# Regrouping the convolution taps, the fold and the norm in the hybrid attentions of a four-layer kernel

## Chip, cores and metric

The kernel runs on one core of one Trainium2 chip. The metric is the device time of one execution in microseconds; a time is the median of several runs. A profile is one execution on the chip, recorded by the hardware.

## What is computed

The reference applies two stacks of two layers each to 1024 tokens of width 1024, all in float32. The change is in the first stack, the hybrid layers. One hybrid layer normalizes its input, projects it to 15 slices, and mixes four groups of 256 channels:

```python
y_a = conformer_conv(a_u, a_v, conv_a_w, conv_a_b, ln_a_g, ln_a_b) * jax.nn.silu(a_z)
y_b = short_gated_conv(b_b, b_c, b_x, conv_b_w) * jax.nn.silu(b_z)
y_c = window_gqa(...) * jax.nn.silu(c_z)
y_d = neighborhood_attn(...) * jax.nn.silu(d_z)
y = jnp.concatenate([y_a, y_b, y_c, y_d], axis=-1)
return x + jnp.einsum("bse,ed->bsd", y, w_out)
```

`conformer_conv` is a depthwise convolution of width 31 over tokens, followed by a layer norm over the 256 channels and a silu. `short_gated_conv` has width 3. `window_gqa` is attention with four query heads over 128 tokens to each side, `neighborhood_attn` attention with four heads over a two-dimensional window of 8 x 16 keys. The second stack (retention, differential attention, feed-forward) is not touched.

## The kernel before

Activations lie channel-major: tiles of 128 channels x 1024 tokens. A float32 matmul operand is split in two parts (`hi`, `lo`), and a product takes three matmuls. `dense` is one projection of 128 output channels: two loads of weights (SP issues the DMA, L202), each split by ScalarE (L205) and GpSimd (L194), then 48 matmuls of 512 columns (L222, L224, L225) into two banks of the ring `pa` of three, which an `evac` function empties. Such a unit needs only the layer's input, so it can stand between other work.

`hybrid` writes one layer in this order: the sliding-window attention `swa`, in which `conv_a` computes the input `h` of the wide convolution for two channel tiles c; the neighbourhood attention `na` for its two pairs of heads; the gate projections; `conv_b`, the short convolution; further gates; the residual and the output projection (`residual`, `hybrid_out`), whose second half needs the normed convolution and `na`'s result.

An attention runs over groups of 256 queries: `swa` has 16 groups, each call of `na` has eight (two heads j, four groups g), so a layer has 32. A group makes scores on TensorE (L507, or L334 and L335) into the two banks `ps`; VectorE adds the mask and takes the maximum (L511, L591); ScalarE takes the exponential (L514, L599); VectorE inverts the sum (L517, L601); GpSimd scales the rows (`scale`, L446). `pv` transposes the rows on TensorE (L416), ScalarE copies them to SBUF (L419), VectorE makes the rest (L420), and TensorE multiplies with the values (L427) into the one bank `po`. `fold` adds the two halves of that bank: a copy on ScalarE (L441), an add on VectorE (L442), and a store by SP (L443).

The wide convolution has 30 taps for each channel tile after its first. For c = 0 a tap is one VectorE instruction over 1024 tokens (L696). For c = 1 it is four pieces of 256 tokens: ScalarE makes a product (L700) in one of two tiles `prod`, and GpSimd adds it (L701). `self.taps` alternates between the two, and `some_taps(n)` writes the next n. `swa` writes three after each group's fold, `na` two. `conv_a_norm` (L716 to L738) writes what taps are left and the layer norm; it is called between the two heads of the second `na`. The pool `cc` has four tiles, for h and the sums of both channel tiles; `conv_b` takes its h and y (L756 to L763) from the same pool.

The order of each engine's queue is not this text's alone. The framework plans the queues at build time, and the order of writing is a rank in that plan:

```python
with tile.TileContext(nc, schedule_with_timeline_sim=True) as tc:
```

At run time each engine works through its queue in the planned order and waits on semaphores.

Of the kernel before, what the change touches and what calls it, by code (L numbers as in the profile page):

```python
# [21 lines left out]
ALU = mybir.AluOpType  # L22
AX = mybir.AxisListType

P = 128
# [39 lines left out]
NPRM = C_FN2 + 8  # L65


NTAP0, NTAP = 3, 2
NGATE = 4
RM = 2  # L70
CPW = 256


class Builder:
    def __init__(self, nc, tc, a, es):
        self.nc, self.tc, self.a, self.es = nc, tc, a, es
        self.n = 0
        self.pools = {}
        self.put_off = None
        self.ready, self.use_ready = [], False  # L80
        self.open(es, cp=1, rp=1, wp=3, xp=13, dp=6, sp=8)
        self.open(es, bass.MemoryType.PSUM, pa=3, ps=2, pt=2, po=1)
        self.open(es, bass.MemoryType.DRAM, dr=2)
# [351 lines left out]

    def fold(self, y, j, g, O):

        nc = self.nc
        m, c = slice(64 * j, 64 * j + 64), slice(64 - 64 * j, 128 - 64 * j)
        t = self.tl("sp", (P, 256), tag="fold", bufs=2)  # L440
        nc.scalar.copy(t[m], O[c, 0:256])  # L441
        nc.vector.tensor_tensor(t[m], O[m, 0:256], t[m], ALU.add)  # L442
        nc.sync.dma_start(y[m, g * 256:(g + 1) * 256], t[m])  # L443

    def scale(self, out, src, colm):
        self.nc.gpsimd.tensor_scalar(out, src, colm, 1.0, ALU.mult, ALU.mult)  # L446
# [23 lines left out]
    def swa(self, l, w):  # L470
        nc = self.nc
# [13 lines left out]
        accs = self.conv_a(l, w)  # L485
        ys = []
        for c in range(2):
# [4 lines left out]
            for j in range(2):  # L492
# [4 lines left out]
                for g in range(4):  # L497
                    p = self.tl("p", (P, 2, 3 * P + 1))
                    nc.vector.tensor_copy(p[:, :, 0], sink.to_broadcast([P, 2]))
                    st = self.st(6)  # L500
                    for e in range(2):
                        i = 2 * g + e
                        k0, k1 = max(i - 1, 0), min(i + 2, NT)
                        n = (k1 - k0) * P
                        ps = self.psS()
                        for m in range(2):
                            nc.tensor.matmul(ps[:, :n], qs[:, j, i * P:(i + 1) * P],  # L507
                                             kk[c][:, m, k0 * P:k1 * P], start=(m == 0),
                                             stop=(m == 1))
                        m0 = (k0 - (i - 1)) * P  # L510
                        nc.vector.tensor_tensor_reduce(  # L511
                            p[:, e, 1:1 + n], ps[:, :n], self.swam[:, m0:m0 + n], -0.125, sink,
                            ALU.add, ALU.min, st[:, e:e + 1])
                        nc.scalar.activation(p[:, e, 0:1 + n], p[:, e, 0:1 + n], AF.Exp,  # L514
                                             scale=-1.0, bias=st[:, e:e + 1],
                                             accum_out=st[:, 2 + e:3 + e])
                    nc.vector.reciprocal(st[:, 4:6], st[:, 2:4])  # L517
                    for e in range(2):
                        i = 2 * g + e
                        n = (min(i + 2, NT) - max(i - 1, 0)) * P  # L520
                        self.scale(p[:, e, 1:1 + n], p[:, e, 1:1 + n], st[:, 4 + e:5 + e])
                    i = 2 * g
                    blocks = [(i, [0, 1]), (i + 1, [0, 1])]
                    if i > 0:
                        blocks.append((i - 1, [0]))
                    if i + 2 < NT:
                        blocks.append((i + 2, [1]))

                    def src(q, kt):
                        o = 1 + (kt - max(i + q - 1, 0)) * P  # L530
                        return p[:, q, o:o + P]

                    O = self.psO()
                    self.pv(O, blocks, src, vops)
                    self.fold(y, j, g, O)
                    self.some_taps(NTAP0)
            ys.append(y)
        return ys, accs


# [16 lines left out]
        nc.vector.memset(t[64:128, 14, :], -BIG)  # L557
        return t

    def na(self, l, w, c, between=None):  # L560
        nc = self.nc
        qf = self.proj(w, 20 + c)
        kf = self.proj(w, 22 + c)
# [2 lines left out]
        V = self.v_pair(vf)  # L566
        y = self.yspill()
        for j in range(2):
            if j and between is not None:
                between()  # L570
            tb = self.na_bias(l, 2 * c + j)
            for g in range(4):
                ps_ = []
# [40 lines left out]
                def src(q, kt):  # L614
                    o = (kt - ps_[q][1]) * P
                    return ps_[q][0][:, o:o + P]

                O = self.psO()
                self.pv(O, blocks, src, V(j))
                self.fold(y, j, g, O)  # L620
                self.some_taps(NTAP)
        return y


# [68 lines left out]
    def tap(self, h, acc, t, w, c):  # L693
        nc = self.nc
# [1 line left out]
            nc.vector.scalar_tensor_tensor(acc, h[:, t:t + S], w, acc, ALU.mult, ALU.add)  # L696
            return
        for i in range(0, S, CPW):
            q = self.tl("sp", (P, CPW), tag="prod", bufs=2)
            nc.scalar.activation(q, h[:, t + i:t + i + CPW], AF.Copy, scale=w)  # L700
            nc.gpsimd.tensor_tensor(acc[:, i:i + CPW], acc[:, i:i + CPW], q, ALU.add)  # L701

# [75 lines left out]
    def hybrid(self, l, last):  # L778
# [3 lines left out]
        with contextlib.ExitStack() as es:  # L782
            self.open(es, pj=4, p=4, tp=4, kl=1, nab=1, cc=4)
            self.open_klo()
            yc, accs = self.swa(l, w)
            yd = [self.na(l, w, 0), self.na(l, w, 1, lambda: self.conv_a_norm(l, accs))]
            gc = [self.gate_spill(w, 18 + c) for c in range(2)]
            yb = self.conv_b(l, w)
            gd = [self.gate_spill(w, 26 + c) for c in range(2)]
            self.spilled = yb  # L790
# [937 lines left out]
```

## Time and profile before

| what | value |
|---|---|
| timed runs | 3733.79 us median of 3 (3724.83 to 3737.05) |
| profiled execution, its own time | 3726.09 us |
| its span, first to last instruction | 3724.3 us |
| mean granted TensorE clock | 0.962 of full speed |
| layer 0: first tap on VectorE, last add of a tap on GpSimd | 97.2 and 298.0 us |

The span is that of the one profiled execution. Times inside it are counted from its first instruction. PE is TensorE's matmul, PEld its weight load, DVE VectorE, ACT ScalarE, POOL GpSimd, SP the queue that issues DMAs. A granted clock of 1.00 is 2.4 GHz, 0.50 is 1.2 GHz.

### The profile page before, as it was taken

How to read it: one execution, taken by the hardware profiler on the slowest of the kernel's cores; microseconds unless marked ns; L12 is line 12 of the kernel's file. 1: busy time of each engine (PE TensorE's matmuls, PEld its weight loads, DVE VectorE, ACT ScalarE, POOL GpSimd, SP SyncE). 2: the span in 40 equal slices, each digit the busy share in tenths (PEclk: the TensorE clock that was granted, in tenths of full speed). 3: DMA queues.
4: the chain of work that ended last, by engine and by line, in shares of the span. 5: the costliest groups of instructions: out<-in, count | busy, mean ns of one | idle time of the engine just before them, and what ended most of it. 6: DMA issues, size and time to landing. Idle time of an engine off the chain costs nothing.

```text
span 3724.3 us, 46324 instructions
## 1 busy us (share of the span) xinstructions
PE 3433.5 (92%) x15872; PEld 2808.6 (75%) x15872; DVE 2531.2 (68%) x3963; ACT 1573.2 (42%) x3207; POOL 2119.8 (57%) x1891
## 2 busy tenths in 40 slices
PE   8899999999999998879999899999997789999898
PEld 6788887788888777667777677887776667777676
DVE  6856647655656655677766899665555586677997
ACT  4475433764444443252333344454433433333333
POOL 4785555874553333466666788533334466666884
PEclk9999999999999998889999999999998889999999
DMA  4112531123422323542122333221236422212432
GB/s 130 36 57 58 177 121 54 39 59 106 156 75 50 52 65 68 149 147 82 68 74 88 119 117 94 88 53 45 48 83 147 122 82 74 96 69 80 144 94 85
DMA packets 186060, 330.40 MB, mean 89 GB/s; under 512 B 49504, under 2 KB 60128, under 8 KB 185824
## 3 DMA queue, kind: packets, MB, share of 16 engines
q1 hardware_dynamic: 185824, 327.44, 29.5%
q8 instruction: 125, 2.05, 0.3%
q14 instruction: 111, 0.91, 0.1%
HBM read 250.23 MB, written 73.99 MB: 87 GB/s over the span
## 4 chain that ended last, share of the span: by engine, by line
PE 60%; DVE 14%; DMA 11%; POOL 7%; issue 4%; ACT 3%; SPq 0%; DVEq 0%; POOLq 0%; ACTq 0%
PE pa L222 9%; PE pa L225 9%; PE pa L224 9%; PE pa L1132 3%; DMA y<-ho 3%; PE pa L1134 3%; PE pa L1135 3%; PE po L427 3%; PE T L1135 3%; PE T L1132 2%; PE T L1134 2%; POOL wlo L194 2%; POOL cc L701 2%; PE ps L1132 2%; PE ps L1135 2%
## 5 line engine op out<-in xcount | busy, mean ns | idle before, releaser
L222 PE MATMUL pa<-xp,whi 128*128 128x512 f32 x2048 | 821.1, 402 | 18.8 <-ACT xp L189 9.9
L224 PE MATMUL pa<-xp,whi 128*128 128x512 f32 x2048 | 820.5, 401 | 8.4 <-DVE xp L190 8.3
L225 PE MATMUL pa<-xp,wlo 128*128 128x512 f32 x2048 | 821.0, 401 | 0.2 <-POOL wlo L194 0.2
L194 POOL TENSOR_TENSOR wlo<-raw,whi 128x512 fp32r<-128x512 f32 x304 | 430.7, 1417 | 447.6 <-ACT whi L205 443.8
L194 POOL TENSOR_TENSOR wlo<-xp,whi 128x512 fp32r<-128x512 f32 x248 | 359.8, 1454 | 190.0 <-ACT whi L1208 189.5
L222 PEld LDWEIGHTS pa<-xp,whi 128*128 128x128 f32 x2048 | 394.2, 193 | 95.5 <-ACT xp L189 10.8
L224 PEld LDWEIGHTS pa<-xp,whi 128*128 128x128 f32 x2048 | 393.3, 192 | 88.4 <-DVE xp L190 14.1
L225 PEld LDWEIGHTS pa<-xp,wlo 128*128 128x128 f32 x2048 | 393.8, 192 | 77.7 <-POOL wlo L194 0.7
L1208 ACT CAST whi<-xp 128x512 fp32r<-128x512 f32 x248 | 153.8, 620 | 405.0 <-PE pa L1134 139.3
L1132 PE MATMUL pa<-xp,whi 128*128 128x512 f32 x672 | 273.8, 407 | 49.8 <-DVE xp L1097 10.9
L205 ACT CAST whi<-raw 128x512 fp32r<-128x512 f32 x304 | 186.9, 615 | 233.8 <-PE pa L224 147.3
L1135 PE MATMUL pa<-xp,wlo 128*128 128x512 f32 x672 | 269.2, 403 | 5.8 <-POOL wlo L194 5.4
L1134 PE MATMUL pa<-xp,whi 128*128 128x512 f32 x672 | 269.5, 401 | 0.0
L446 POOL TENSOR_SCALAR p<-p,st 128x256 f32<-128x256 f32 (+4 forms) x224 | 157.3, 710 | 196.1 <-DVE st L991 94.2
L701 POOL TENSOR_TENSOR cc<-cc,prod 128x256 f32<-128x256 f32 x240 | 199.8, 854 | 30.0 <-ACT prod L700 23.8
L1132 PEld LDWEIGHTS pa<-xp,whi 128*128 128x128 f32 x672 | 130.8, 195 | 91.9 <-issue 19.6
L420 DVE TENSOR_TENSOR tp<-T,tp 128x512 fp32r<-128x512 f32 (+2 forms) x224 | 132.2, 599 | 97.4 <-ACT tp L419 96.4
L334 PE MATMUL ps<-xp,xp 128*128 128x512 f32 (+4 forms) x384 | 144.1, 376 | 37.7 <-DVE p L932 31.9
L427 PE MATMUL po<-tp,xp 128*128 128x256 f32 (+1 forms) x1024 | 166.5, 283 | 12.4 <-ACT tp L419 11.3
L427 PEld LDWEIGHTS po<-tp,xp 128*128 128x128 f32 x1024 | 151.3, 193 | 33.3 <-ACT tp L419 16.2
L700 ACT ACTIVATE prod<-cc,c 128x256 f32<-128x256 f32 x240 | 119.0, 507 | 108.8 <-POOL cc L701 97.3
L986 ACT ACTIVATE p<-p,st 128x384 f32<-128x384 f32 (+3 forms) x192 | 117.1, 611 | 111.8 <-DVE st L979 110.2
(316 smaller groups left out, 8241.4 us busy)
## 6 DMA issues: line engine op xcount, KB each, us to landing
raw<-w_in SPq DMA_DIRECT2D x208, 256.0 KB, 2.9
xp<-x SPq DMA_DIRECT2D x48, 512.0 KB, 6.8
xp<-w_gate SPq DMA_DIRECT2D x44, 512.0 KB, 5.2
xp<-w_up SPq DMA_DIRECT2D x44, 512.0 KB, 5.1
raw<-w_out SPq DMA_DIRECT2D x80, 256.0 KB, 3.3
x<-xp SPq DMA_DIRECT2D x80, 256.0 KB, 2.2
h<-xp SPq DMA_DIRECT2D x40, 512.0 KB, 2.9
xp<-h SPq DMA_DIRECT2D x80, 256.0 KB, 4.4
```

The lines of the kernel that those rows point to most:

```text
L194: self.last_rest = self.nc.gpsimd.tensor_tensor(lo, src, hi.bitcast(F32), ALU.subtract)
L205: nc.scalar.copy(hi, raw)
L222: nc.tensor.matmul(ps[h], hi[:, k - k0, :], x[:, 0, t], start=(k == 0), stop=False)
L224: nc.tensor.matmul(ps[h], hi[:, k - k0, :], x[:, 1, t], start=False, stop=False)
L225: nc.tensor.matmul(ps[h], lo[:, k - k0, :], x[:, 0, t], start=False, stop=(k == nk - 1))
L427: nc.tensor.matmul(O[:, qs[0] * P:qs[0] * P + w], lhsT, pt[part][:, o:o + w], start=((kt, qs) == blocks[0] and i == 0), stop=((kt, qs) == ...
L446: self.nc.gpsimd.tensor_scalar(out, src, colm, 1.0, ALU.mult, ALU.mult)
L701: nc.gpsimd.tensor_tensor(acc[:, i:i + CPW], acc[:, i:i + CPW], q, ALU.add)
L1132: nc.tensor.matmul(ps, hi[:, k, :], xh, start=(start and k == 0), stop=False, skip_group_check=True)
L1134: nc.tensor.matmul(ps, hi[:, k, :], xl, start=False, stop=False, skip_group_check=True)
L1135: nc.tensor.matmul(ps, lo[:, k, :], xh, start=False, stop=(k == len(ops) - 1), skip_group_check=True)
L1208: self.nc.scalar.copy(hi, src)
```

## The change

Both attentions write two taps a group instead of three and two, and write them between the scaling and `pv` instead of after the fold. `fold` writes only ScalarE's copy; the add and the store are kept back and written by `fold_rest` ahead of the next group's `pv`, or at the end of the attention. The norm moves from between the heads of the second `na` to behind the first two gates. The product tiles become four. The same instructions are written, in another order.

```diff
@@ -65,7 +65,7 @@
 NPRM = C_FN2 + 8
 
 
-NTAP0, NTAP = 3, 2
+NTAP = 2
 NGATE = 4
 RM = 2
 CPW = 256
@@ -77,6 +77,7 @@
         self.n = 0
         self.pools = {}
         self.put_off = None
+        self.fold_off = None
         self.ready, self.use_ready = [], False
         self.open(es, cp=1, rp=1, wp=3, xp=13, dp=6, sp=8)
         self.open(es, bass.MemoryType.PSUM, pa=3, ps=2, pt=2, po=1)
@@ -435,12 +436,22 @@
 
     def fold(self, y, j, g, O):
 
+
         nc = self.nc
         m, c = slice(64 * j, 64 * j + 64), slice(64 - 64 * j, 128 - 64 * j)
         t = self.tl("sp", (P, 256), tag="fold", bufs=2)
         nc.scalar.copy(t[m], O[c, 0:256])
-        nc.vector.tensor_tensor(t[m], O[m, 0:256], t[m], ALU.add)
-        nc.sync.dma_start(y[m, g * 256:(g + 1) * 256], t[m])
+
+        def rest():
+            nc.vector.tensor_tensor(t[m], O[m, 0:256], t[m], ALU.add)
+            nc.sync.dma_start(y[m, g * 256:(g + 1) * 256], t[m])
+
+        self.fold_off = rest
+
+    def fold_rest(self):
+        if self.fold_off is not None:
+            self.fold_off()
+        self.fold_off = None
 
     def scale(self, out, src, colm):
         self.nc.gpsimd.tensor_scalar(out, src, colm, 1.0, ALU.mult, ALU.mult)
@@ -530,11 +541,13 @@
                         o = 1 + (kt - max(i + q - 1, 0)) * P
                         return p[:, q, o:o + P]
 
+                    self.some_taps(NTAP)
+                    self.fold_rest()
                     O = self.psO()
                     self.pv(O, blocks, src, vops)
                     self.fold(y, j, g, O)
-                    self.some_taps(NTAP0)
             ys.append(y)
+        self.fold_rest()
         return ys, accs
 
 
@@ -557,7 +570,7 @@
         nc.vector.memset(t[64:128, 14, :], -BIG)
         return t
 
-    def na(self, l, w, c, between=None):
+    def na(self, l, w, c):
         nc = self.nc
         qf = self.proj(w, 20 + c)
         kf = self.proj(w, 22 + c)
@@ -566,8 +579,6 @@
         V = self.v_pair(vf)
         y = self.yspill()
         for j in range(2):
-            if j and between is not None:
-                between()
             tb = self.na_bias(l, 2 * c + j)
             for g in range(4):
                 ps_ = []
@@ -615,10 +626,12 @@
                     o = (kt - ps_[q][1]) * P
                     return ps_[q][0][:, o:o + P]
 
+                self.some_taps(NTAP)
+                self.fold_rest()
                 O = self.psO()
                 self.pv(O, blocks, src, V(j))
                 self.fold(y, j, g, O)
-                self.some_taps(NTAP)
+        self.fold_rest()
         return y
 
 
@@ -696,7 +709,7 @@
             nc.vector.scalar_tensor_tensor(acc, h[:, t:t + S], w, acc, ALU.mult, ALU.add)
             return
         for i in range(0, S, CPW):
-            q = self.tl("sp", (P, CPW), tag="prod", bufs=2)
+            q = self.tl("sp", (P, CPW), tag="prod", bufs=4)
             nc.scalar.activation(q, h[:, t + i:t + i + CPW], AF.Copy, scale=w)
             nc.gpsimd.tensor_tensor(acc[:, i:i + CPW], acc[:, i:i + CPW], q, ALU.add)
 
@@ -783,8 +796,9 @@
             self.open(es, pj=4, p=4, tp=4, kl=1, nab=1, cc=4)
             self.open_klo()
             yc, accs = self.swa(l, w)
-            yd = [self.na(l, w, 0), self.na(l, w, 1, lambda: self.conv_a_norm(l, accs))]
+            yd = [self.na(l, w, 0), self.na(l, w, 1)]
             gc = [self.gate_spill(w, 18 + c) for c in range(2)]
+            self.conv_a_norm(l, accs)
             yb = self.conv_b(l, w)
             gd = [self.gate_spill(w, 26 + c) for c in range(2)]
             self.spilled = yb
```

## Rows read from the trace of the kernel before

**Rows 1.** The page: busy time, share, instructions of each engine.

```profile
PE 3433.5 (92%) x15872; PEld 2808.6 (75%) x15872; DVE 2531.2 (68%) x3963; ACT 1573.2 (42%) x3207; POOL 2119.8 (57%) x1891
```

**Rows 2.** Busy us by stage: stretch, its length, engines (instructions), clock, DMA.

```profile
core 0: us, PE busy (x) PEld busy (x) DVE busy (x) ACT busy (x) POOL busy (x), PEclk, DMA share, GB/s
125.00:200.00 75.00, 65.24 (x321) 53.03 (x320) 53.61 (x103) 48.10 (x116) 69.30 (x76) 0.98 0.12 34
...
200.00:400.00 200.00, 199.58 (x1072) 169.72 (x1071) 114.90 (x263) 124.43 (x269) 129.21 (x161) 1.00 0.24 67
...
625.00:710.00 85.00, 74.56 (x367) 61.18 (x367) 61.98 (x116) 51.80 (x124) 74.14 (x79) 0.98 0.11 33
```

**Rows 3.** The same view in windows of 10 us.

```profile
140.00:150.00 10.00, 6.63 (x23) 5.03 (x23) 7.71 (x12) 5.22 (x14) 9.72 (x10) 0.83 0.13 34
...
190.00:200.00 10.00, 9.59 (x51) 7.86 (x50) 6.88 (x17) 7.08 (x20) 8.04 (x12) 1.00 0.14 39
...
650.00:660.00 10.00, 7.61 (x33) 6.25 (x34) 7.73 (x16) 5.13 (x14) 9.72 (x8) 0.83 0.10 31
```

**Rows 4.** Timeline of TensorE: start, us, what, idle before and releaser.

```profile
138.69 0.39 PE L225 MATMUL pa<-xp,wlo 128*128 128x512 f32 x1
...
139.83 0.39 PE L224 MATMUL pa<-xp,whi 128*128 128x512 f32 x1
...
142.46 0.77 PE L507 MATMUL ps<-xp,xp 128*128 128x256 f32 x2 [2.24 <-DVE st L511]
...
143.02 0.63 PE L225 MATMUL pa<-xp,wlo 128*128 128x512 f32 x1
```

**Rows 5.** Waits from 125 to 200: us in total, times, longest.

```profile
ACT prod L700 <- POOL cc L701: 27.7, 24, 3.1
DVE st L517 <- ACT p L514: 9.9, 7, 2.9
...
PE ps L507 <- DVE st L511: 6.2, 4, 2.4
...
DVE fold L442 <- ACT fold L441: 5.6, 3, 3.0
...
PE po L427 <- ACT tp L419: 2.5, 2, 1.4
```

**Rows 6.** Chain of waits from 125 to 176, shares by line.

```profile
by line: POOL cc L701 46.3%; POOL p L446 26.0%; POOL wlo L194 14.2%; issue 6.6%; DVE cc L696 3.2%; ACT prod L700 2.8%; ACT p L514 1.2%; DVE p L511 1.0%; POOLq L194 0.2%; DVE st L511 0.0%
```

**Rows 7.** Source lines: count, ns min/median/max, first and last start.

```profile
L696 DVE SCALAR_TENSOR_TENSOR cc<-cc,c,cc x30: 1264/1285/2315, 97.2 to 167.1; 128x1024 f32<-128x1024 f32 x30
...
L701 POOL TENSOR_TENSOR cc<-cc,prod x120: 719/741/1772, 123.1 to 298.0; 128x256 f32<-128x256 f32 x120
...
L441 ACT COPY fold<-po x6: 364/370/371, 143.6 to 197.4; 64x256 f32<-64x256 f32 x6
```

**Rows 8.** GpSimd's busy us of L701 alone, then of L446 alone (twice).

```profile
125.00:200.00 75.00, 40.69 (x46) 0.98 0.12 34
...
125.00:200.00 75.00, 18.50 (x20) 0.98 0.12 34
...
200.00:300.00 100.00, 13.13 (x20) 1.00 0.20 57
```

**Rows 9.** Source line of the fold's add in layer 0.

```profile
L442 DVE TENSOR_TENSOR fold<-po,fold x32: 394/422/429, 144.0 to 478.4; 64x256 f32<-64x256 f32 x32
```

**Rows 10.** Source lines: norm, residual, output, second convolution (both layers).

```profile
L716 PE MATMUL T<-cc,c x8: 590/592/595, 394.2 to 401.8; 128*128 128x512 f32 x8
...
L738 DVE SCALAR_TENSOR_TENSOR cc<-p,cc x4: 671/676/692, 414.7 to 433.7; 128x512 f32<-128x512 f32 x4
...
L822 DVE TENSOR_TENSOR xp<-pa,xp x16: 672/684/692, 438.0 to 489.4; 128x512 f32<-128x512 f32 x16
...
L838 DVE TENSOR_TENSOR xp<-pa,xp x16: 691/692/692, 492.1 to 532.9; 128x512 f32<-128x512 f32 x16
...
L761 ACT ACTIVATE cc<-cc,c x4: 1152/1153/1157, 299.5 to 836.5; 128x1024 f32<-128x1024 f32 x4
```

**Rows 11.** Groups of TensorE from 298 to 394: count, busy us, mean ns.

```profile
L225 PE MATMUL pa<-xp,wlo 128*128 128x512 f32 x97 | 38.4, 396 | 0.0
```

## The prediction

> **What bounds the kernel now.** The page first: TensorE is busy for 92% of the span [rows 1], so a change that adds and removes no arithmetic can only win what TensorE stands still or runs slowly. The profiled execution took 3726.09 us with a span of 3724.3; the three timed runs have a median of 3733.79, 7.7 above it. I make the sum against 3726.09 and carry the difference to the median. A change under 0.3% (11.2 us) can't be told from none here.
>
> Next, busy time by stage of the two hybrid layers [rows 2]. In layer 0 TensorE is busy for 65.24 of the 75 us from 125 to 200, then for 199.58 of 200. Layer 1 repeats it: 74.56 of 85 from 625 to 710. So of all that the diff touches, only the first groups of the sliding-window attention have idle to give: 9.76 and 10.44 us, 20.2 together. In that stretch GpSimd is busy for 69.30 of 75.
>
> The finer windows [rows 3] show the clock as well: 0.83 granted in 140 to 150 and in 650 to 660, where TensorE stands still for 3.37 and 2.39 us. In the timeline, matmuls of 512 columns take 0.39 us before a 2.24 us stop and 0.63 behind it [rows 4]: 2.4 GHz, then 1.2 for a while. That is 0.17 x 10 = 1.7 us per layer, 3.4 in all.
>
> Then who is waited for there [rows 5]. TensorE waits 6.2 us for VectorE's masked maximum (L511, the reader of the score banks) and 2.5 for ScalarE's copy of a transpose (L419). VectorE waits 9.9 for the exponential (L514), and ScalarE waits 27.7 us, 24 times, in L700, the product of a tap, for GpSimd's add L701 to give back one of two product tiles. Engines run their queues in order, so an exponential or a copy behind L700 waits too. The chain of waits from 125 to 176 agrees: 46.3% L701, 26.0% the scaling L446, 14.2% the weight split L194 [rows 6]. GpSimd's queue sets the pace of these groups.
>
> **The change, part by part.** No instruction is added or removed: 30 taps on VectorE and 30 on ScalarE and GpSimd (120 products, 120 adds) per layer remain.
>
> *Taps, three to two a group in the sliding window.* Taps alternate between the channels, so three a group are on average 1.5 x 4 = 6 adds, two are 4. Six fold copies lie in 125 to 200 [rows 7], five intervals of a group; the last ends in 190 to 200, where GpSimd is busy for only 8.04 of 10 [rows 3]. That leaves four intervals in which it sets the pace: 4 x 2 = 8 adds fewer ahead of the scalings. An add costs 40.69 / 46 = 0.885 us in this stretch [rows 8]. 8 x 0.885 = 7.1 us per layer, 14.2 for two. The bounds: nothing, if the queues are ordered by what is ready and the adds stay where they are; and all idle and slow clock, 20.2 + 3.4 = 23.6. I take 14.2, which leaves the clock uncounted, since one stop left over can keep it slow. What goes out comes back later: the window's 16 groups give up 16 taps to the neighbourhood attention, eight of them on GpSimd: 32 adds, or 24 us at the 0.741 us of the median one [rows 7]. The cover there is TensorE's full queue: from 200 to 400 GpSimd is busy for only 129.21 of 200 us [rows 2]. Uncovered they would cost those 24.
>
> *Four product tiles.* ScalarE may run two more products ahead: 2 x 0.74 = 1.5 us of slack, against waits of 27.7 / 24 = 1.2 us on average, 3.1 at most [rows 5]. I count nothing for it: it frees ScalarE, not GpSimd, which is the pace. Its bounds are the whole ScalarE part, already within 23.6, and the loss in the third rival.
>
> *Fold in two steps.* VectorE's add (0.42 us, 32 a layer) and its store go behind the next group's scores [rows 9]. VectorE waits 5.6 us in this stretch for the fold copy [rows 5], standing in front of L511; that wait overlaps the same stops, so it is not added. Nothing to 2 x 5.6 us. What is late: the single output bank is released later, so the next group's value matmuls (L427) can wait behind the add; a group's interval of about 10 us hides 0.42. On SP the stores move past weight loads, 32 a layer; SP is no step of the chain [rows 6], and their readers come a stage later, so nothing; were a weight load held up by a store that waits for the add, the price is that add's lateness, a group at most. The fold has two tiles, and one is held a group longer, with as much slack.
>
> *Norm behind the gates.* It now stands behind both halves of the second neighbourhood attention instead of between them. Its matmuls start at 394.2 and its last VectorE step at 433.7 [rows 10], 40 us of chain. The cover is the residual's dense work, whose evacuations run from 438.0 to 489.4, before the first of the output's at 492.1 [rows 10]. If the two change places, the norm ends about where attention now ends, at 478.4 [rows 9]. The output's first matmuls, 24 x 0.228 = 5.5 us ahead of their evacuation, need it by 487. I take nothing; each us past that is lost once per layer, 40 at the most without cover.
>
> **Sum.** 3726.1 - 14.2 = 3711.9 for an execution like the profiled one; against the median 3733.8 - 14.2 = 3719.6, say 3720.
>
> **Rivals.** *Same: GpSimd stays the pace, because VectorE's taps slow it.* All 30 VectorE taps are issued between 97.2 and 167.1, while the sixth group is folded at 197.4 [rows 7]; in program order six groups hold 18 taps, nine of them VectorE's. So instructions are placed by readiness, and the written place of a tap hardly counts. While those taps run, GpSimd's work stretches: 20 scalings take 18.50 us against 13.13 for 20 in the next 100 us [rows 8], though some of the latter are wider; 46 adds take 40.69 against 34.1 at the median [rows 7, 8]. That is 5.4 + 6.6 = 12 us per layer, more than the whole idle. If this is the cause, moving GpSimd's taps wins nothing: 3734. By the Trainium skill, page "SBUF — State Buffer", section "Who interferes with whom", a VectorE instruction with two inputs in SBUF contends with a GpSimd one that reads SBUF, and whichever issues second waits for the first to finish. The 18.50 against 13.13 us [rows 8] agree with it. Against the rival: taps on GpSimd are limited by product tiles and follow the groups at four to six adds each, and fewer of them make the same slowing rarer.
>
> *Slower: the last tap comes late, and TensorE lacks work to fill with.* The second convolution's first result L761 starts at 299.5, right behind the last add at 298.0 [rows 7, 10]: it needs the tile that the taps hold. Two of its six dense units are written ahead of that result; the other four come behind and fill TensorE. In program order the last tap moves from the 22nd of 32 groups to the 30th, past 394. From 298 to 394 dense matmuls run on three lines, 98, 97 and 97 of them [rows 11], 66.6 us at the 0.228 us from one to the next (139.83 - 138.69 over five) [rows 4]. Without the four units, four gate units that depend on nothing remain (4 x 48 x 0.228 = 43.8 us). That covers until about 298 + 96 x 43.8 / 66.6 = 361; past it each us costs 0.69 per layer. At 394 that is 23 us, two layers 45; I price it at half, 3734 + 22 = 3756. Against it: GpSimd's idle after 200 [rows 2] draws the adds forward.
>
> *Slower: four product tiles let more adds in.* If GpSimd's plan had gaps only for want of products, two more tiles put two more adds into each of four intervals: the same 14.2 us with the other sign, 3748. It decides from the 46 adds in 125 to 200 upwards. For it: ScalarE is busy for only 48.10 of 75 [rows 2] and could make them. Against it: GpSimd had 5.7 us free there, and six adds become ones of lower rank.
>
> **Chances.** The forecast 0.52, with its own range 3710 (all idle and clock) to 3727 (half of the adds); the part under 11.2 us of gain takes 0.07. Same 0.27, late last tap 0.09, more adds 0.12. So faster 0.45, within 0.3% 0.34, slower 0.21. The range reaches from 3704, all idle gone from the lowest run shown (3724.83 - 20.2), to 3748, the third rival; outside it lies the late last tap and little else.
>
> **What would show it.** Right: fewer than 40 adds in the 75 us after the first one, TensorE's idle there under 4 us per layer, ScalarE's wait in L700 under 10, no clock of 0.83, the last add still before 360, and no idle between 487 and 495. Wrong: the scalings still at 18.50 / 20 = 0.9 us with VectorE taps beside them and the same 9 to 10 us idle; or idle that turns up between 300 and 500 where there is none; or TensorE waiting in L427 for the fold's add.

## The result and the profile after

The changed kernel took 3762.87 us (median of 4 runs, 3756.28 to 3770.24), the kernel before 3731.39 beside it (4 runs, 3724.83 to 3737.05): ratio 1.0085, 95% interval [1.0056, 1.0115]. The forecast was 3720, so the change is slower where a gain was expected, and the time lies above the range. The profiled execution took 3756.28 us with a span of 3754.5.

The page of the changed kernel, busy time of each engine, answers to [rows 1]:

```profile
PE 3435.6 (92%) x15872; PEld 2806.5 (75%) x15872; DVE 2575.1 (69%) x3963; ACT 1572.4 (42%) x3207; POOL 2110.5 (56%) x1891
```

The counts are the same and TensorE's work is, too. VectorE alone grew, by 43.9 us with the same 3963 instructions: some of them last longer. That is the line to follow.

Busy time by stage, in the stretches of [rows 2]:

```profile
125.00:200.00 75.00, 63.55 (x309) 51.13 (x309) 55.48 (x97) 48.59 (x116) 70.87 (x81) 0.98 0.11 33
200.00:400.00 200.00, 192.11 (x1029) 164.79 (x1028) 126.29 (x266) 118.09 (x259) 122.58 (x156) 0.98 0.22 62
625.00:710.00 85.00, 74.54 (x347) 60.14 (x346) 71.59 (x100) 45.30 (x106) 66.91 (x65) 0.98 0.11 34
```

TensorE's idle in the first groups is not gone: 11.45 us against 9.76. The new loss is in the second line: 7.89 us of idle between 200 and 400, where there were 0.42, and a clock of 0.98 instead of 1.00. In finer windows the worst slice is this one:

```profile
260.00:270.00 10.00, 6.77 (x30) 5.78 (x29) 6.91 (x9) 5.88 (x14) 6.54 (x10) 0.79 0.25 87
```

The layers end (the start of the first copy of the next scale, R) at 564.6 and 1099.4 us instead of 548.3 and 1068.0: 16.3 and 15.1 us a layer. Together that is 31.4 us, as much as the medians differ by, 31.5; the two profiled spans differ by 30.2, so the second stack adds nothing in them. In layer 0 the 16.3 are, stretch by stretch, 9.2 us more idle in 120 to 290 (19.34 against 10.18), 3.2 of idle between 460 and 500, and the clock of 0.96 in 200 to 290, 0.04 x 82.1 busy us = 3.3: 15.7.

Waits between 125 and 200 (total, times, longest), beside [rows 5], and the chain from 125 to 176, beside [rows 6]:

```profile
ACT prod L713 <- POOL cc L714: 25.4, 21, 3.4
...
DVE fold L446 <- ACT fold L443: 7.7, 4, 3.0
...
PE ps L518 <- DVE st L522: 4.4, 3, 2.6
```

```profile
by line: POOL cc L714 57.2%; POOL wlo L195 18.2%; POOL p L457 11.0%; issue 5.0%; DVE cc L709 3.2%; ACT p L525 2.1%; ACT whi L206 2.0%; ACT prod L713 1.8%; DVE p L522 1.0%; DVE st L522 0.0%
```

ScalarE still waits for product tiles, though it has twice as many. GpSimd's adds hold 57.2% of the chain, not 46.3%: they came in larger numbers, and earlier. Source lines (ns min/median/max, first and last start) and GpSimd's time in the adds and in the scalings alone, beside [rows 7] and [rows 8]:

```profile
L709 DVE SCALAR_TENSOR_TENSOR cc<-cc,c,cc x30: 1267/1285/2311, 97.3 to 168.0; 128x1024 f32<-128x1024 f32 x30
...
L714 POOL TENSOR_TENSOR cc<-cc,prod x120: 720/742/1782, 123.2 to 283.5; 128x256 f32<-128x256 f32 x120
```

```profile
125.00:200.00 75.00, 45.65 (x51) 0.98 0.11 33
...
125.00:200.00 75.00, 13.02 (x20) 0.98 0.11 33
```

There are 51 adds in the 75 us where there were 46, and the last starts at 283.5 instead of 298.0. The written place of the taps moved towards the end, yet the adds moved to the front. The scalings took 13.02 us instead of 18.50: GpSimd itself is not what got worse.

Where VectorE's time went is seen in the groups of 120 to 290 (busy us, mean ns, idle before) and the timeline around 200, VectorE first, then GpSimd, then TensorE:

```profile
L510 DVE COPY p<-c 128x2 f32<-128x2 f32 x12 | 14.2, 1187 | 2.3 <-PE T L417 2.1
L644 DVE SCALAR_TENSOR_TENSOR dp<-dp,dp 128x512 f32<-128x512 f32 x4 | 9.2, 2296 | 2.0 <-ACT dp L643 2.0
```

```profile
199.62 5.12 DVE L510 COPY p<-c 128x2 f32<-128x2 f32 x1
204.75 0.62 DVE L522 CUSTOM_DVE_ANT_0 p<-ps,c,c 128x384 f32<-128x384 f32 x1
...
198.17 1.15 POOL L457 TENSOR_SCALAR p<-p,st 128x384 f32<-128x384 f32 x2
199.28 4.21 POOL L714 TENSOR_TENSOR cc<-cc,prod 128x256 f32<-128x256 f32 x6
203.45 1.26 POOL L195 TENSOR_TENSOR wlo<-raw,whi 128x512 fp32r<-128x512 f32 x1
206.60 0.74 POOL L714 TENSOR_TENSOR cc<-cc,prod 128x256 f32<-128x256 f32 x1 [1.89 <-ACT prod L713]
...
202.24 0.40 PE L225 MATMUL pa<-xp,whi 128*128 128x512 f32 x1
205.43 0.62 PE L518 MATMUL ps<-xp,xp 128*128 128x384 f32 x2 [2.79 <-DVE st L522]
```

Read it from the copy. Line 510 copies the sink, two columns, and its shortest takes 0.154 us. Here it lasts 5.12 us and ends at 204.74, when GpSimd has done six adds and a weight split without a pause (203.45 + 1.26 = 204.71). Behind it in VectorE's queue stands the masked maximum L522, which frees the score banks, and TensorE waits 2.79 us for it. The same picture stands at 236.37 (3.41 us) and, with the gate's L644, at 256.73 (6.71 us, shortest 0.68); at 177.72 a rotation's add, L312, lasts 4.26 instead of 1.22. These four alone make some 17 us of VectorE's time. In the kernel before, no sink copy lasts over 1.02 us, and the same stretch of GpSimd's queue, here in its later profile b0_before_again, pauses after every few adds, because ScalarE's next product, or its part of a weight split, is not there yet:

```profile
195.97 2.13 POOL L701 TENSOR_TENSOR cc<-cc,prod 128x256 f32<-128x256 f32 x3
198.73 1.44 POOL L701 TENSOR_TENSOR cc<-cc,prod 128x256 f32<-128x256 f32 x2 [0.64 <-ACT prod L700]
200.51 1.29 POOL L194 TENSOR_TENSOR wlo<-raw,whi 128x512 fp32r<-128x512 f32 x1 [0.34 <-ACT whi L205]
```

Between 125 and 280 GpSimd pauses for more than 0.15 us 18 times in the kernel before and 6 times in the changed one. A run without a pause is not enough for a long wait, though. In the kernel before GpSimd works from 257.0 to 276.9 without one, and the two casts that VectorE makes inside it last 1.03 and 1.15 us against 0.69. In the changed kernel GpSimd works so from 123.2 to 180.9, and no VectorE tap lasts over 2.31 us against 1.27.

### The profile page after: what moved, and what is told of

It is laid out like the page before. It is cut to its first block, busy times and chain, and to the rows that moved or that the text cites. A ratio compares the mean times of both kernels' runs of the same rounds, so it can differ in the third digit from the quotient of the medians.

```text
span 3754.5 us, 46377 instructions
## 1 busy us (share of the span) xinstructions
PE 3435.6 (92%) x15872; PEld 2806.5 (75%) x15872; DVE 2575.1 (69%) x3963; ACT 1572.4 (42%) x3207; POOL 2110.5 (56%) x1891
## 4 chain that ended last, share of the span: by engine, by line
PE 57%; DVE 16%; DMA 12%; POOL 8%; issue 4%; ACT 3%; SPq 0%; DVEq 0%; POOLq 0%; ACTq 0%
PE pa L223 8%; PE pa L226 8%; PE pa L225 8%; PE pa L1146 3%; PE pa L1148 3%; PE pa L1149 3%; POOL cc L714 3%; DMA y<-ho 3%; PE T L1149 3%; PE po L428 2%; PE T L1146 2%; PE T L1148 2%; POOL wlo L195 2%; PE ps L1146 2%; PE ps L1149 2%
## 5 line engine op out<-in xcount | busy, mean ns | idle before, releaser
L457 POOL TENSOR_SCALAR p<-p,st 128x256 f32<-128x256 f32 (+4 forms) x224 | 145.9, 659 | 223.1 <-DVE st L1005 92.7
L428 PE MATMUL po<-tp,xp 128*128 128x256 f32 (+1 forms) x1024 | 168.1, 284 | 22.8 <-ACT tp L420 16.7
L428 PEld LDWEIGHTS po<-tp,xp 128*128 128x128 f32 x1024 | 153.3, 194 | 44.0 <-ACT tp L420 20.9
L1241 POOL TENSOR_TENSOR xp<-xp,R 128x512 f32<-128x512 f32 x80 | 111.1, 1388 | 84.0 <-DVE xp L1240 84.0
```

Source lines behind the costliest of these rows:

```text
L428: nc.tensor.matmul(O[:, qs[0] * P:qs[0] * P + w], lhsT, pt[part][:, o:o + w], start=((kt, qs) == blocks[0] and i == 0), stop=((kt, qs) == ...
```

## The experiments

Runs were made on more than one chip, and the kernel before took from 3704.55 to 3731.39 us on them, so every ratio is to its runs beside the experiment. "Idle" is TensorE's between 120 and 290 in layer 0: 10.18 us before, 19.34 after. "Layers end" is the end of the second hybrid layer: 1068.0 and 1099.4. "Adds" are GpSimd's adds between 125 and 200 as the windows count them: 46 and 51.

### Which part costs

The first experiment is the change with two product tiles, the second the kernel before with four:

```diff
 # e1_change_two_tiles: the changed kernel
-            q = self.tl("sp", (P, CPW), tag="prod", bufs=4)
+            q = self.tl("sp", (P, CPW), tag="prod", bufs=2)
 # e2_before_four_tiles: the kernel before
-            q = self.tl("sp", (P, CPW), tag="prod", bufs=2)
+            q = self.tl("sp", (P, CPW), tag="prod", bufs=4)
```

> The changed kernel with two product tiles instead of four. Theory A (with four tiles GpSimd's adds follow each other without a gap, and a VectorE instruction that reads SBUF waits until the run of adds ends): the long VectorE instructions go, the copy of the sink back from at most 5.1 us to about 1, TensorE's idle from 120 to 290 falls from 19 to about 11 us per layer, the time by 15 to 25 us from 3763, to about 3740. Theory B (the place of the taps and of the fold is the cause): 3755 to 3765, with the idle as it is.

> The kernel before with four product tiles and nothing else. Theory A: 15 to 25 us slower than before, 3746 to 3757, with VectorE instructions of 3 us and more between 190 and 290, and the last add some 10 us earlier. Theory B: within 6 us of before, 3731.

Measured: e1 1.0036 [1.0025, 1.0047], idle 10.8, layers end at 1071.5; e2 1.0072 [1.0059, 1.0086], idle 19.4, layers end at 1098.3. Stages and the sink copy's group in 120 to 290, first of e1, then of e2:

```profile
120.00:200.00 80.00, 69.64 (x341) 56.92 (x340) 58.05 (x112) 49.10 (x118) 71.87 (x78) 0.98 0.11 35
200.00:290.00 90.00, 89.59 (x478) 75.55 (x477) 47.90 (x110) 69.43 (x157) 79.18 (x103) 1.00 0.17 55
...
L510 DVE COPY p<-c 128x2 f32<-128x2 f32 x12 | 4.8, 403 | 0.7 <-PE T L417 0.7
L644 DVE SCALAR_TENSOR_TENSOR dp<-dp,dp 128x512 f32<-128x512 f32 x4 | 3.1, 772 | 3.3 <-ACT dp L643 3.3
```

```profile
120.00:200.00 80.00, 68.56 (x332) 55.32 (x331) 60.46 (x106) 50.42 (x122) 73.50 (x81) 0.98 0.11 34
200.00:290.00 90.00, 82.02 (x421) 69.86 (x420) 58.11 (x105) 64.58 (x151) 78.88 (x102) 0.96 0.17 53
...
L499 DVE COPY p<-c 128x2 f32<-128x2 f32 x12 | 13.7, 1146 | 2.2 <-PE T L416 2.1
L631 DVE SCALAR_TENSOR_TENSOR dp<-dp,dp 128x512 f32<-128x512 f32 x4 | 9.2, 2293 | 2.0 <-ACT dp L630 2.0
```

One number, 2 or 4, carries the whole picture from one kernel to the other: the idle, the clock of 0.96, the long copies. The four tiles cost 0.7% by themselves, and the taps' place has no part in it.

That number also gives the framework another plan. Each engine's instructions, read in order from the traces up to 300 us, stand in e1 as in the kernel before and in e2 as in the changed kernel, but for one add and one scaling of GpSimd that change places. From two tiles to four all four engines' orders differ: ahead of the fourth pair of scalings, for example, GpSimd has 22 adds instead of 17. So e1 and e2 show that the number of tiles costs; they don't tell the run-time room for products from the new order.

Next, the norm: in e3 the changed kernel has it between the heads again, in e4 only the norm moves in the kernel before, n1 is e4 once more, and n2 puts it ahead of the gates.

```diff
 # e4_before_norm_moved, n1_norm_moved_again: the kernel before (e3_change_norm_back: the reverse, in the changed one)
-            yd = [self.na(l, w, 0), self.na(l, w, 1, lambda: self.conv_a_norm(l, accs))]
+            yd = [self.na(l, w, 0), self.na(l, w, 1)]
             gc = [self.gate_spill(w, 18 + c) for c in range(2)]
+            self.conv_a_norm(l, accs)
 # n2_norm_before_gates: the same, with conv_a_norm ahead of the line of gc
```

> The changed kernel with the norm back between the heads of the second neighbourhood attention. Theory N (the norm now stands last before the output, and TensorE waits for it): the 3.2 us of TensorE's idle between 460 and 500 in layer 0 and 1.6 in layer 1 go, the time falls by 4 to 9 us from 3763. Otherwise no difference beyond 3 us.

> The kernel before with only the norm moved behind the gates. Theory N: 4 to 9 us slower than before, with TensorE idle ahead of the output projection. If the norm is covered: within 3 us of before.

> The kernel before with only the norm moved, a second time. If the 15 us of the first time belong to the move: 10 to 18 us slower than before again. If they came from how the clock was granted in the second stack, which the trace of the first time shows: 0 to 6 us, since the hybrid layers themselves ended only 2.4 us later.

> The kernel before with the norm written directly behind the second neighbourhood attention, ahead of the two gates. If the place in the plan counts (the norm's VectorE work now lies among the residual's evacuations): the norm's matmuls start no later than 433 and the loss is smaller than in the run beside it, or the same when the plan doesn't change.

Measured: e3 1.0070 [1.0054, 1.0086], layers end at 1091.1; e4 1.0040 [1.0025, 1.0056] and n1 1.0015 [1.0006, 1.0024], the same kernel twice, layers end at 1070.0 and 1071.7; n2 1.0019 [1.0010, 1.0027], 1073.4. The moved norm costs something, 0.15 to 0.4%; the two measurements of it don't agree, and the hybrid layers in their traces lose only 2.4 and 4.1 us to the 1067.6 of a further profile of the kernel before (b0_before_again, below). The rest of e4's 0.4% lies behind them, where nothing was moved; that stays open.

### Parts that change nothing in the queues

In e5 the taps alone are moved (two a group, ahead of `pv`), in e6 the fold alone is split, and e7 has both: the changed kernel with two product tiles and the norm between the heads.

```diff
 # e5_before_taps_moved: the kernel before, in swa; in na the line moves likewise
+                    self.some_taps(NTAP)
                     O = self.psO()
                     self.pv(O, blocks, src, vops)
                     self.fold(y, j, g, O)
-                    self.some_taps(NTAP0)
 # e6_before_fold_split: the kernel before, with fold and fold_rest of the change
+                    self.fold_rest()
                     O = self.psO()
```

> The kernel before with only the taps moved: two a group, ahead of the transposes, with two product tiles. My prediction: 14 us faster than before, with some 8 adds fewer from 125 to 200. Theory A (GpSimd's adds are placed by what is ready, held back by the product tiles alone): within 4 us of before, 46 adds give or take two, the last add at 298.

> The kernel before with only the fold in two steps. If the fold's add in front of the masked maximum holds up TensorE: 2 to 8 us faster. If the output bank that is released later costs: 2 to 8 us slower, with TensorE waiting for the fold's add. Theory A: within 3 us.

> The changed kernel with two product tiles and the norm back, so taps and fold alone differ from before. Theory A and N together: within 4 us of before; if taps and fold are the win that was predicted, 10 to 15 us faster, and if they cost by themselves, slower.

Measured: e5 1.0001 [0.9991, 1.0011], e6 0.9997 [0.9986, 1.0007], e7 1.0002 [0.9993, 1.0012]. GpSimd's adds in e5, in 125 to 200 and in the whole layer:

```profile
125.00:200.00 75.00, 41.94 (x44) 0.93 0.11 33
...
L701 POOL TENSOR_TENSOR cc<-cc,prod x120: 712/740/2077, 125.2 to 300.6; 128x256 f32<-128x256 f32 x120
```

Two fewer than 46, where the prediction had eight fewer, and in no less time (41.94 us against 40.69). Even the two are no effect: the adds run from 125.2 to 300.6 instead of 123.1 to 298.0, because in this trace everything comes some 2 us later. The order hardly moved. In both hybrid layers e6 has the same order of instructions on GpSimd, VectorE and ScalarE as the kernel before, and in e5 and e7 one add and one scaling change places on GpSimd in each layer. So these runs don't show that the parts are worth nothing once they take place: the framework's plan came out the same with them.

### The dose, and the copy

The kernel before with three tiles and with one; and the changed kernel with the sink copied by ScalarE:

```diff
 # t3_before_three_tiles, t1_before_one_tile: the kernel before
-            q = self.tl("sp", (P, CPW), tag="prod", bufs=2)
+            q = self.tl("sp", (P, CPW), tag="prod", bufs=3)   # t1: bufs=1
 # l1_change_sink_on_scalar: the changed kernel
-                    nc.vector.tensor_copy(p[:, :, 0], sink.to_broadcast([P, 2]))
+                    nc.scalar.copy(p[:, :, 0], sink.to_broadcast([P, 2]))
```

> The kernel before with three product tiles. Theory A (the longer the unbroken runs of adds, the longer VectorE is kept out): between two tiles and four, 8 to 20 us slower than before, the longest copy of the sink between 1 and 5 us. If only the fourth tile counted, within 4 us.

> The changed kernel with the sink's copy, the small instruction that waited up to 5.1 us on VectorE, given to ScalarE; four product tiles stay. If VectorE's lock-out is what costs TensorE its time: the 9 us by which these copies grew per layer go, and TensorE's idle from 120 to 290 falls by 3 to 8 us per layer; the time by 6 to 15 us from the change's. If the earlier adds alone are the cause (GpSimd's queue fuller ahead of the scalings): within 4 us of the change, +31.

> The kernel before with one product tile. If the number of tiles sets how many adds stand in a row and with it VectorE's waits (14 us of sink copies at four tiles, 12 at three, 4 at two), one tile has no add right behind another: fewer than 44 adds in 125 to 200, sink copies under 4 us, idle of 5 to 10 us there, ratio 0.997 to 1.000, unless the last add moves past 340 and leaves TensorE without work at 300 to 400, which would make it slower by up to 0.5%. If tiles cost by something else, such as the place of tiles in SBUF, ratio within 0.1% of 1.

Measured: t3 1.0027 [1.0017, 1.0037], idle 14.2, longest sink copy 4.33 us (and a cast of 7.28), layers end at 1085.1. With 2, 3 and 4 tiles the cost goes 0, 0.27, 0.72%, while GpSimd's pauses over 0.15 us between 125 and 280 go 18, 9, 6. Each number of tiles has a plan of its own here too, and so has l1. l1: 1.0052 [1.0038, 1.0066], idle 15.4, layers end at 1088.9: a part of the cost goes with the copy; other VectorE instructions are shut out in its place (a cast for 5.54 us, the gate's L644 for 6.36).

t1: 1.0054 [1.0034, 1.0074], layers end at 1090.4, and the last add of layer 0 starts at 372.4 instead of 298.0. Stages of layer 0, and the adds of 125 to 200:

```profile
120.00:200.00 80.00, 73.25 (x373) 59.16 (x372) 64.16 (x123) 46.66 (x114) 62.49 (x66) 1.00 0.12 36
200.00:290.00 90.00, 90.00 (x483) 77.24 (x482) 54.33 (x121) 61.88 (x137) 66.74 (x81) 1.00 0.21 60
290.00:400.00 110.00, 102.99 (x533) 85.37 (x532) 58.29 (x140) 63.41 (x134) 66.71 (x89) 0.92 0.20 56
...
125.00:200.00 75.00, 29.59 (x32) 1.00 0.12 35
```

With 32 adds instead of 46 the first groups do get better (6.75 us of idle between 120 and 290), and the price comes back at 290 to 400, where 7.01 us of idle and a clock of 0.92 stand in place of none. That is the prediction's rival of the late last tap, in a kernel where the taps really are late. Its GpSimd pauses 45 times. Two tiles lie between two losses.

### How long VectorE is shut out

A probe behind the end of the kernel before: one GpSimd add lets a VectorE copy of 128x2 go, and k further adds follow it. In p1 the copy follows the add directly; in p2 a ScalarE copy stands between, so that it arrives inside the run. Five times each it reads SBUF, then PSUM (times of the whole kernel mean nothing here).

```diff
 # p2_copy_into_run_of_adds; in p1 the ScalarE copy is missing and VectorE reads a constant
+        for e in (self.sm(2), ps):
+            for k in (0, 1, 2, 4, 8):
+                nc.gpsimd.tensor_tensor(u[:, h], x[:, h], d[:, h], ALU.add)
+                for i in range(k):
+                    t = slice(i % 2 * 256, i % 2 * 256 + 256)
+                    nc.gpsimd.tensor_tensor(y[:, t], y[:, t], u[:, h], ALU.add)
+                nc.scalar.copy(e[:, 0:2], u[:, 0:2])
+                nc.vector.tensor_copy(d[:, 0:2], e[:, 0:2])
```

> The kernel before with a probe behind its end: ten times, GpSimd makes one add that lets a VectorE copy of 128x2 go, and 0, 1, 2, 4 or 8 further adds of 128x256 right behind it; five times the copy reads SBUF and five times it reads PSUM. Theory (VectorE is shut out until GpSimd's unbroken run ends): the copy from SBUF lasts about 0.2 us with no add behind, and about 0.7, 1.4, 2.9 and 5.8 us with 1, 2, 4 and 8. Rival (it waits only for the one instruction that is under way): at most 0.9 us whatever the number. For the copy from PSUM I expect 0.2 us throughout if only the read from SBUF counts, the same stairs if its write to SBUF counts too.

> The probe behind the end of the kernel before once more, with ScalarE between: GpSimd's first add lets a ScalarE copy of two columns go, and that lets the VectorE copy of 128x2 go, so that it arrives some 0.3 to 0.5 us into the 0, 1, 2, 4 or 8 further adds (0.68 us each), instead of ahead of them as in the first probe. Five times the VectorE copy reads SBUF, five times PSUM. Theory (shut out for the whole unbroken run): from SBUF it ends with the run, so it lasts about 0.2, 0.4, 1.1, 2.4 and 5.2 us. Rival (it waits for the one add that is under way): at most 0.9 us for any number. From PSUM: 0.2 us throughout if only the read from SBUF counts; the same stairs if the write to SBUF counts too.

In p1 all ten copies took 0.16 to 0.17 us: they started 0.04 us ahead of the run and met none of it, so p1 tells nothing of the question. p2, the timeline with eight adds, reading SBUF and then PSUM:

```profile
3729.19 5.48 POOL L1637 TENSOR_TENSOR dp<-dp,dp 128x256 f32<-128x256 f32 x8
3729.37 0.57 DVE L1639 COPY dp<-sm 128x2 f32<-128x2 f32 x1 [3.07 <-ACT sm L1638]
...
3744.26 5.48 POOL L1637 TENSOR_TENSOR dp<-dp,dp 128x256 f32<-128x256 f32 x8
3744.41 0.16 DVE L1639 COPY dp<-T 128x2 f32<-128x2 f32 x1 [3.48 <-ACT T L1638]
```

With 1, 2, 4 and 8 adds behind it the copy from SBUF took 0.57 us each time, and each time it arrived inside the first of them. A single add takes 0.72, so the first ends at 3729.91 and the copy at 3729.94: it waits for the add under way and is let in there. From PSUM it never waits. So my theory, shut out until the run ends, falls as a rule, and the rival holds in the probe. The changed kernel shows both: of the 20 sink copies of its two hybrid layers that lasted over 0.25 us beside GpSimd's work, 15 end 22 to 32 ns behind the GpSimd instruction that was under way, one behind the next, and four (at 199.62, 236.37 and their like in layer 1) only when five or seven instructions had gone by and GpSimd paused. What decides whether a waiting copy is let in between two instructions stays open; the four come at the same two places of both layers, so it is no accident of one run.

### What is left in the kernel before

VectorE's taps left out (v1), the sink copied by ScalarE with two tiles (s1), VectorE's taps tied to the eighth group (g1; until then two of GpSimd's taps are written a group, and the pool `cc` has a fifth tile), and the kernel before itself once more for its trace (b0).

```diff
 # v1_before_no_vector_taps: the kernel before
         if c == 0:
-            nc.vector.scalar_tensor_tensor(acc, h[:, t:t + S], w, acc, ALU.mult, ALU.add)
             return
 # s1_before_sink_on_scalar: the kernel before, with l1's line
 # g1_before_vector_taps_later, in part: the kernel before; first() is the write that acc for c = 0 begins with
+                    if 8 * c + 4 * j + g == 7:
+                        b = self.tl("sp", (P, 1), tag="gate", bufs=1)
+                        nc.vector.tensor_scalar(b, st[:, 0:1], 0.0, self.col(C_CB + 2 * l),
+                                                ALU.mult, ALU.add)
+                        self.first(b)
```

> The kernel before, unchanged, for a trace on the chip of the runs it stands beside: the hybrid layers end at about 1068 us as in the first trace, TensorE idle about 10 us from 120 to 290. If the second stack differs by more than 5 us from the first trace, a comparison of whole spans between traces is worth no more than that.

> The kernel before without VectorE's 30 taps per layer for c = 0 (they are left out, so the convolution of these channels has one tap instead of 31). If VectorE's taps are what slows GpSimd in the first groups (the prediction's rival Same), 20 scalings in 125 to 200 take 13 to 15 us instead of 18.5, TensorE's idle there falls from 10 us to under 5 and the time by 0.15 to 0.35%. If they are not, the idle stays at 8 to 11 us and the ratio at 0.999 to 1.001.

> The kernel before, with its two product tiles, and the copy of the sink made by ScalarE instead of VectorE. If the shut-out needs runs of adds, as with more product tiles, there is little to win here: the 12 copies of 125 to 290 took 4.2 us in all, so at most 2 us per layer, ratio 0.9985 to 1.0005. If the sink copy itself is the costly place at any number of tiles, the idle of 10 us falls to about 6 and the ratio to 0.997 to 0.998.

> The kernel before with VectorE's taps tied to the eighth sliding-window group: the first of them gets its bias from a column that needs that group's maximum, so all 30 run after it, where TensorE has a full queue (the pool of the convolution gets a fifth tile, so that the second convolution needn't wait for theirs). If VectorE's taps beside GpSimd's full queue are what stops TensorE in the first groups, the idle of 125 to 200 falls from 10 to under 4 us per layer and, if nothing comes back later, the ratio is 0.994 to 0.998. If the contention only moves along with the taps, idle of some 10 us turns up between 200 and 330 and the ratio is 0.999 to 1.004.

b0: layers end at 1067.6, idle 10.4, 47 adds: the first stack of [rows 2] over again; its second stack's two layers differ by 6 and 15 us from the first trace's. s1: 0.9991 [0.9981, 1.0002], no difference. v1: 0.9932 [0.9916, 0.9948], layers end at 1042.1. Its stages, and its scalings in 125 to 200:

```profile
120.00:200.00 80.00, 80.00 (x427) 69.18 (x426) 48.34 (x116) 62.47 (x150) 69.73 (x93) 1.00 0.15 44
200.00:290.00 90.00, 90.00 (x488) 77.38 (x488) 53.04 (x118) 67.57 (x152) 81.14 (x100) 1.00 0.20 58
...
125.00:200.00 75.00, 12.77 (x24) 1.00 0.15 43
```

No idle at all, with more adds than before (53), and a scaling takes 12.77 / 24 = 0.53 us instead of 18.50 / 20 = 0.93. The idle that the change went for hangs on VectorE's taps, not on the number of GpSimd's. v1 leaves out VectorE's own 38.6 us a layer (30 x 1.285) as well as their collisions with GpSimd, and doesn't part the two.

g1: 1.0077 [1.0059, 1.0094], layers end at 1094.1:

```profile
120.00:200.00 80.00, 75.65 (x388) 63.58 (x386) 58.22 (x107) 53.84 (x126) 74.49 (x85) 1.00 0.13 39
200.00:290.00 90.00, 76.16 (x372) 60.19 (x372) 63.94 (x109) 54.52 (x127) 85.26 (x87) 0.98 0.15 48
```

VectorE's taps now start between 158.3 and 260.0, and the idle moves with them, from the first stretch (4.35 us) to the second (13.84), and grows. No version here beats the kernel before with the same output.

## Why the prediction was wrong

**What bounds the kernel** was read rightly as to place (the first groups have the only idle) and half rightly as to cause. The chain named GpSimd's adds, and I took their number for the pace. v1 has more of them and no idle; t1 has 14 fewer and keeps 6.75 us of it.

**Taps, three to two a group: the step that failed first.** I took 14.2 us from eight adds fewer in four intervals of each layer, as if the place in which a tap is written were its place in the queue. The lower bound that I named, that the queues are ordered by what is ready and the adds stay where they are, is what happened: in e5 17 adds stand ahead of the fourth pair of scalings, as before, and the ratio is 1.0001. The evidence stood in my own rows: all VectorE taps done by 167 while six groups end at 197 [rows 7]. I used it for a rival of 0.27 and not for the sum.

**Four product tiles: the step that made it a loss.** "I count nothing for it: it frees ScalarE, not GpSimd, which is the pace." It cost 0.72% (e2), 27 us, and nearly all of what the change lost: e1 takes it out and comes back to 1.0036, e7 without the norm to 1.0002. ScalarE's wait for tiles, 27.7 us [rows 5], looked like lost time; in the kernel before it goes with pauses in GpSimd's queue. With four tiles GpSimd pauses less often (6 times instead of 18), and a VectorE instruction that reads SBUF can stand 3 to 7 us behind it, with the score banks' reader queued behind that.

The third rival had the cause (the tiles), the place, the sign and the direction of the adds (46 to 51), and its 14.2 us was half the size. Its mechanism, adds ahead of the scalings, is there (22 instead of 17 ahead of the fourth pair), but cost little: the 20 scalings of 125 to 200 took 13.02 us and the idle there grew by 1.7. Most of the loss lies behind 200, in waits that it did not name. That the lost time is VectorE's waiting is read from the traces, in which the four longest instructions of layer 0 answer for some 17 us and TensorE waits for the maximum behind them. That they are so long because the pauses are fewer is argued from the timelines and the dose, and not shown; p2 and the unbroken runs of both kernels bound it: a VectorE instruction is not shut out by every run. The rival that the plan's new order by itself brings instructions together in a worse way is untested, since no run has four tiles in the old order.

By the Trainium skill, page "SBUF — State Buffer", section "Who interferes with whom", VectorE and GpSimd share a pair of ports, whoever issues first has it for the whole instruction, and copies in some modes take it as well as instructions with two SBUF inputs. p2 agrees (0.57 us from SBUF until the add ends, 0.16 from PSUM), and so do 15 of the 20 sink copies; four that waited through five or seven instructions go past it. I cited this rule in the prediction for VectorE's taps slowing GpSimd and did not turn it round.

**Same: VectorE's taps.** The rival was right about the term that it contradicted: moving GpSimd's taps wins nothing, and without VectorE's taps the idle and the slow scalings are gone (v1). The slow scalings alone were a weak sign: the changed kernel has the same 30 taps in the same stretch, and its scalings took 13.02 us, too.

**Fold in two steps** came out as nothing (e6), but not by the overlap that I argued: the queues did not change, so neither the gain nor the late bank was put to the test. **Norm behind the gates** was mis-sized: nothing was counted, and it cost 0.15 to 0.4%. The cover that I named, the residual's dense work, was not whole: the norm's small steps and the residual's evacuations stand in one VectorE queue. Where the norm alone moves, TensorE waits there for 1.24 us in layer 0 (e4) and 1.40 (n1), behind two norm steps of some 1.67 us. In the changed kernel it waits longer in one place, 1.72 us, but there four sink copies stand ahead of the evacuation, two of them shut out for 1.28 and 1.27 us. First e4, then the changed kernel:

```profile
474.82 1.67 DVE L738 SCALAR_TENSOR_TENSOR cc<-p,cc 128x512 f32<-128x512 f32 x1
476.41 0.68 DVE L823 TENSOR_TENSOR xp<-pa,xp 128x512 f32<-128x512 f32 x1
...
477.14 0.50 PE L222 MATMUL pa<-xp,whi 128*128 128x512 f32 x1 [1.24 <-DVE xp L823]
```

```profile
485.11 2.61 DVE L510 COPY p<-c 128x2 f32<-128x2 f32 x4
...
489.06 0.47 PE L223 MATMUL pa<-xp,whi 128*128 128x512 f32 x1 [1.72 <-DVE xp L836]
```

**The late last tap** did not come: the last add moved forward, to 283.5. t1 shows that its mechanism is real.

Of the signs named ahead, fewer than 40 adds, idle under 4 us and ScalarE's wait under 10 all failed (51, 11.45, 25.4). "No clock of 0.83" held at 140 to 150 and failed at 260 to 270 (0.79), behind the longest shut-out; "no idle between 487 and 495" failed by the 1.72 us above. Of the signs against, idle turned up between 300 and 500 (3.2 us), and TensorE waited once in L428, the new number of L427, for the fold's add, 0.9 us between 125 and 200; e2, whose fold is not split, has the same wait.

## What to carry to other kernels

A wait in front of a small ring of buffers may be what leaves gaps for a third engine (argued here, not shown), and a deeper ring can cost (0.27 and 0.72%); before deepening the ring, look at who shares a resource with the consumer, and at the longest single durations of small instructions (max far from median), not at the sum of waits. Where a framework plans the queues, the written place of independent work may move nothing (the same order and 1.0001 here), while one buffer more reorders every engine: compare the order of the queues before you credit an edit with anything. Take a many-part change apart early: here the parts that were argued longest changed nothing in the queues, and one digit cost 0.7%.

## What was not expected of the hardware

A VectorE copy of two columns, 0.154 us at its shortest, lasted 5.12 us beside seven GpSimd instructions in a row, at the same place in both layers (5.116 and 5.108), while the same kind of copy in p2 got in behind the first of eight adds. The second stack of the kernel before took 2656.3 us in its first profile and 2635.5 in b0, a later one, with nothing changed in it; the runs were made on more than one chip.
